# High and low products in runs, and the bias rows by way of DRAM: a two-layer decoder trunk

## The chip, the core and the metric

The kernel runs on one core of a Trainium2 chip. The metric is the device time of one execution in microseconds. Five engines work side by side, each through its own queue in order: PE multiplies matrices (with PEld, its weight loads), DVE and ACT do elementwise work, POOL small things, SP and ACT issue DMAs. All weights come from HBM, 173 MB in one execution.

## The reference, cut to what matters

Two layers, 256 positions, width 1024. Each layer is a half-step feed-forward, a mixer of three head groups, and a second half-step feed-forward:

```
def swiglu(x, w_gate, w_up, w_down):
    return (jax.nn.silu(x @ w_gate) * (x @ w_up)) @ w_down      # 1024 -> 2816 -> 1024

for l in range(DEPTH):                                          # DEPTH = 2
    h = x + 0.5 * swiglu(rms_norm(x, ffn1_norm[l]), ffn1_gate[l], ffn1_up[l], ffn1_down[l])
    u = rms_norm(h, mix_norm[l]);  z = u @ w_in[l]
    ...                       # differential attention, short convolution, RG-LRU
    h = h + jnp.concatenate([y_da, y_sc, y_lru], axis=-1) @ w_out[l]
    x = h + 0.5 * swiglu(rms_norm(h, ffn2_norm[l]), ffn2_gate[l], ffn2_up[l], ffn2_down[l])
return rms_norm(x, final_norm)
```

The attention adds a bias to its logits that depends on the distance of query and key alone: `rel_bias[t5_bucket(distance)]`, eight heads' worth.

## The kernel before

**Split products.** Every float32 operand is split into a high part (rounded to the matrix engine's format) and a low part, the rest. A product is then high by high, high by low and low by high. ACT makes a weight chunk's high part `wh` (line 161), DVE its low part `wl` by subtraction (line 165), each in two halves of four contraction tiles; the activations lie in `xx` (feed-forward input) and `hid` (hidden), high and low side by side, so that one matmul with `wh` and 512 columns takes both, and one with `wl` and 256 columns takes the high half alone. `wide` (line 219) issues this pair for one contraction tile k: first `wh`, then `wl`, and for the last tile of a sum in the other order. The 512 result columns are added afterwards.

**Stages.** A feed-forward has 22 chunks for gate and up in turn (`up_gate`, line 311), each with two output columns a and b (`ga`, `gb`, `ua`, `ub`) of eight tiles k, by `wide_col` (line 228): 44 columns of 16 matmuls in a pass, four passes in all. Three of the four then go through `ffn` (line 380): four blocks n of two columns `da`, `db`, each over 22 tiles k that come in three chunks of 8, 8 and 6 tiles. The mixer's projections (`col`, line 213) are in 256-column matmuls throughout, and the last down projection (`row`, line 840) in matmuls of 512 and of 256 columns, each kind in a row.

**Order.** The schedule is by hand: each engine gets its instructions in the order in which the Python code issues them. `chunk` (line 196) and `pump` (line 190) keep ACT and DVE some chunks ahead of PE with four buffers of `wh` and of `wl`, and SP's loads three ahead of those.

**Bias.** Hooks run behind chunk pair c of the first pass (line 808). Hook 2, `bias_rows`, makes the eight bias rows of 384 values (`br`, on 8 partitions of SBUF). Hook 7, `skew_out`, writes each row 128 times into DRAM (`skew`, 1536 KB) from ACT's queue; hook 9, `skew_in`, reads it back with a shifted stride into `bias`, which the attention needs much later. An instruction behind `skew_in` on ACT cannot start before ACT has waited for `skew` to land.

Of the kernel before, what the change touches and what calls it, by code (L numbers as in the profile page):

```python
# [11 lines left out]
F32 = mybir.dt.float32  # L12
# [5 lines left out]
P = 128  # L18
DEPTH = 2
S = 256  # L20
D = 1024
KD = D // P
DFF = 2816
KF = DFF // P
# [45 lines left out]
def trunk(ctx: ExitStack, tc: tile.TileContext, t, out):  # L70
    nc = tc.nc
# [7 lines left out]
    dr = ctx.enter_context(tc.tile_pool(name="dr", bufs=1, space=bass.MemoryType.DRAM))  # L79
# [4 lines left out]
    def pair(name):  # L84
        return [bank(name + "a"), bank(name + "b")]
# [4 lines left out]
    def flat(ap):  # L90
        return ap.rearrange("p a b -> p (a b)")
# [10 lines left out]
    xx = cst.tile([P, KD, 2, S], F32R, name="xx")  # L102
# [5 lines left out]
    bias = cst.tile([P, 8, S], F32, name="bias")  # L108
# [12 lines left out]
    for l in range(DEPTH):  # L121
        for f in ("ffn1", "ffn2"):
# [3 lines left out]
            w = t[f"{f}_down{l}"]  # L126
# [69 lines left out]
    def chunk(held=0):  # L196

        n = st["use"]
        st["live"] = n - held
        while st["split"] < 2 * (n + 1):  # L200
            split_half()
        low_to(2 * (n + 1))
        load_to(n + LS + LD)
        st["use"] += 1
        return parts.pop(n)
# [10 lines left out]
        for k in ks:  # L216
            mm3(o, w[0][:, k - k0, c], w[1][:, k - k0, c], vh[:, k], vl[:, k], k == first, k == last)

    def wide(o, wh, wl, v, first, last):

        if last:
            nc.tensor.matmul(o[:, :S], lhsT=wl, rhs=v[:, 0], start=first, stop=False)
            nc.tensor.matmul(o, lhsT=wh, rhs=flat(v), start=False, stop=True)
        else:
            nc.tensor.matmul(o, lhsT=wh, rhs=flat(v), start=first, stop=False)  # L225
            nc.tensor.matmul(o[:, :S], lhsT=wl, rhs=v[:, 0], start=False, stop=False)  # L226

    def wide_col(o, w, i, ks):
        c = slice(i * P, (i + 1) * P)
        for k in ks:  # L230
            wide(o, w[0][:, k, c], w[1][:, k, c], xx[:, k], k == 0, k == KD - 1)

    def fresh_cols(norm, b, column):

# [145 lines left out]
    def ffn(norm, first, gain, hooks=()):  # L380
        hid = up_gate(norm, first, hooks)
        for n in range(4):
            acc = pair("d")
            for k0, k1 in DOWN_K:
                w = chunk()
                for i in range(2):
                    c = slice(i * P, (i + 1) * P)
                    for k in range(k0, k1):
                        wide(acc[i], w[0][:, k - k0, c], w[1][:, k - k0, c], hid[k], k == 0, k == KF - 1)
                    if k1 == KF:  # L390
                        settle(2 * n + i, acc[i], gain, norm)
                    if n < 3 or k1 < KF or i == 1:
                        pump()


    kept = {}
# [63 lines left out]
    def bias_rows():  # L460
# [2 lines left out]
        kept["br"] = wk.tile([8, 384], F32, tag="at", name="br")  # L463
        nc.vector.tensor_copy(out=kept["br"], in_=b[:8, :384])

    def skew_out():
        kept["skew"] = dr.tile([8, P, 384], F32, name="skew")
        nc.scalar.dma_start(out=kept["skew"], in_=kept["br"].unsqueeze(1).to_broadcast([8, P, 384]))

    def skew_in():  # L470
        sk = kept["skew"][:]
        nc.scalar.dma_start(
            out=bias, in_=bass.AP(sk.tensor, sk.offset + P - 1, [[383, P], [P * 384, 8], [1, S]])
        )


    def mixer(l, norm):
# [327 lines left out]
        nc.gpsimd.tensor_tensor(out=xq, in0=junk[:, 0], in1=junk[:, 1], op=ALU.add)  # L805

    norm = Norm()
    ffn(norm, True, ("mix_norm", 0), {1: constants_in, 2: bias_rows, 4: exponents, 5: softplus, 6: factors, 7: skew_out, 9: skew_in})
    for l in range(DEPTH):
        norm = Norm()  # L810
        mixer(l, norm)
        norm = Norm()
        if l < DEPTH - 1:
            ffn(norm, False, ("ffn1_norm", l + 1))
            norm = Norm()
# [13 lines left out]
    hid = up_gate(norm, False, {2 + 2 * k + n: turn_back(k, n) for k in range(2) for n in range(2)})  # L829
# [7 lines left out]
    acc = (f0, f1 + [bank("f2")])  # L837
# [41 lines left out]
    for c in range(NC - 2):  # L879
        w = chunk()  # L880
# [4 lines left out]
    w = [chunk(), chunk(1)]  # L885
# [45 lines left out]
```

## Time and profile before

| | |
|---|---|
| median of 3 runs | 963.83 us (963.38 to 964.7) |
| the profiled execution | 963.61 us |
| its span, first to last instruction | 961.5 us |
| PE busy | 950.6 us, 99% of the span |
| DVE, ACT busy | 682.7 us (71%), 548.8 us (57%) |
| matmuls, all of them | 5894 |

A matmul's busy time contains its way through the pipeline (a 512-column one shows about 0.40 us though the next begins after 0.23), so a busy PE says only that it never ran dry. How fast it goes is read from the distance between the starts of successive matmuls, best over whole columns, whose times stand with two decimals. The two kinds of matmul are called h (with `wh`, 512 columns) and l (with `wl`, 256 columns) from here on.

### The profile page before, as it was taken

The page shows a single profiled execution, that of the slowest core. Times are in us where ns is not written, and L with a number is a line of the kernel's source. Part 1 is how long each engine was busy: PE and PEld are TensorE (multiplying, and loading weights), DVE is VectorE, ACT ScalarE, POOL GpSimd, SP SyncE. Part 2 cuts the span into 40 slices and gives each one's busy share as a digit, 9 for nine tenths or more (in the row PEclk, how much of TensorE's full clock was granted, in tenths as well). Part 3 has the DMA queues.
Part 4 walks back from the last instruction along what each step waited for, and adds up shares of the span by engine and source line. Part 5 has one row for each costly group of instructions (what it writes and reads, how often), then busy time and mean ns, then how long its engine had stood idle before and what let it go on. Part 6 is the DMA issues. An engine that isn't in the chain of part 4 may idle for free.

```text
span 961.5 us, 14717 instructions
## 1 busy us (share of the span) xinstructions
PE 950.6 (99%) x5894; PEld 849.5 (88%) x5894; DVE 682.7 (71%) x1018; ACT 548.8 (57%) x935; POOL 27.5 (3%) x49
## 2 busy tenths in 40 slices
PE   8999999999999999999999999999999999999997
PEld 7888878899999888888888888888999988888886
DVE  6788647767787877765678777575778777777643
ACT  7467436557766655554556555454677666555431
POOL 2003000000000000000000000000000000000000
PEclk9999999999999999999999999999999999999999
DMA  7665767554445655553646554454633555555721
GB/s 275 233 217 178 180 213 254 170 190 155 140 167 176 219 180 197 192 193 131 241 145 220 200 186 165 164 199 173 218 133 132 176 194 200 176 176 181 277 89 44
DMA packets 29671, 176.67 MB, mean 184 GB/s; under 512 B 4227, under 2 KB 6308, under 8 KB 10404
## 3 DMA queue, kind: packets, MB, share of 16 engines
q1 hardware_dynamic: 25632, 171.45, 51.2%
q10 hardware_dynamic: 3972, 4.29, 2.1%
q8 instruction: 46, 0.75, 0.3%
q14 instruction: 21, 0.17, 0.1%
HBM read 173.11 MB, written 2.62 MB: 183 GB/s over the span
## 4 chain that ended last, share of the span: by engine, by line
PE 79%; DVE 7%; DMA 5%; ACT 5%; issue 2%; POOL 1%; ACTq 0%; SPq 0%; POOLq 0%; DVEq 0%
PE db L225 6%; PE da L225 6%; PE gb L225 6%; PE ub L225 6%; PE ua L225 6%; PE ga L225 6%; DMA skew<-br 4%; PE db L226 3%; PE da L226 3%; PE ga L226 3%; PE ua L226 3%; PE gb L226 3%; PE ub L226 3%; DVE wl L165 3%; ACT wh L161 2%
## 5 line engine op out<-in xcount | busy, mean ns | idle before, releaser
L165 DVE TENSOR_TENSOR wl<-raw,wh 128x1024 fp32r<-128x1024 f32 (+2 forms) x334 | 390.6, 1196 | 63.5 <-ACT wh L161 63.2
L161 ACT ACTIVATE wh<-raw 128x1024 fp32r<-128x1024 f32 (+2 forms) x334 | 325.4, 1021 | 49.1 <-PE f L211 21.1
L225 PE MATMUL ga<-xx,wh 128*128 128x512 f32 x308 | 111.9, 401 | 0.8 <-DVE xx L307 0.8
L225 PE MATMUL gb<-xx,wh 128*128 128x512 f32 x308 | 111.3, 399 | 0.0
L225 PE MATMUL ub<-xx,wh 128*128 128x512 f32 x308 | 110.7, 399 | 0.0
L225 PE MATMUL ua<-xx,wh 128*128 128x512 f32 x308 | 110.3, 397 | 0.0
L225 PE MATMUL da<-hid,wh 128*128 128x512 f32 x252 | 89.8, 394 | 0.4 <-ACT wh L161 0.4
L225 PE MATMUL db<-hid,wh 128*128 128x512 f32 x252 | 89.8, 395 | 0.0
L226 PE MATMUL ga<-xx,wl 128*128 128x256 f32 x308 | 87.2, 283 | 0.8 <-DVE wl L165 0.8
L226 PE MATMUL gb<-xx,wl 128*128 128x256 f32 x308 | 86.6, 281 | 0.0
L226 PE MATMUL ua<-xx,wl 128*128 128x256 f32 x308 | 86.5, 281 | 0.0
L226 PE MATMUL ub<-xx,wl 128*128 128x256 f32 x308 | 86.3, 280 | 0.0
L226 PE MATMUL da<-hid,wl 128*128 128x256 f32 x252 | 70.8, 281 | 1.7 <-DVE wl L165 1.7
L226 PE MATMUL db<-hid,wl 128*128 128x256 f32 x252 | 70.6, 280 | 0.0
L225 PEld LDWEIGHTS ga<-xx,wh 128*128 128x128 f32 x308 | 58.4, 189 | 13.5 <-ACT wh L161 1.0
L225 PEld LDWEIGHTS gb<-xx,wh 128*128 128x128 f32 x308 | 58.2, 189 | 12.4
L225 PEld LDWEIGHTS ub<-xx,wh 128*128 128x128 f32 x308 | 57.9, 188 | 12.1
L225 PEld LDWEIGHTS ua<-xx,wh 128*128 128x128 f32 x308 | 58.0, 188 | 11.8
L226 PEld LDWEIGHTS ga<-xx,wl 128*128 128x128 f32 x308 | 58.6, 190 | 3.5 <-DVE wl L165 2.0
L335 ACT ACTIVATE sg<-sg 128x512 f32<-128x512 f32 x44 | 27.8, 633 | 57.7 <-DVE sg L334 57.7
L226 PEld LDWEIGHTS gb<-xx,wl 128*128 128x128 f32 x308 | 58.5, 190 | 1.8
L226 PEld LDWEIGHTS ub<-xx,wl 128*128 128x128 f32 x308 | 58.2, 189 | 1.9
(313 smaller groups left out, 1988.3 us busy)
## 6 DMA issues: line engine op xcount, KB each, us to landing
raw<-in_ffn_up SPq DMA_DIRECT2D x43, 1024.0 KB, 4.8
raw<-in_ffn_gate SPq DMA_DIRECT2D x42, 1024.0 KB, 4.7
raw<-in_ffn_down SPq DMA_DIRECT2D x35, 1024.0 KB, 4.8
raw<-in_w_in SPq DMA_DIRECT2D x22, 1024.0 KB, 4.8
raw<-in_ffn_down SPq DMA_DIRECT2D x12, 768.0 KB, 4.1
raw<-in_w_out SPq DMA_DIRECT2D x8, 1024.0 KB, 4.8
skew<-br ACTq DMA_DIRECT2D x1, 1536.0 KB
xT<-in_x SPq DMA_DIRECT2D x4, 256.0 KB, 4.9
```

Source lines behind the costliest of these rows:

```text
L161: nc.scalar.activation(out=parts[i][0][:, s], in_=raws[i][:, s], func=AF.Copy)
L165: nc.vector.tensor_tensor(out=lo[:, s], in0=raws[i][:, s], in1=h[:, s].bitcast(F32), op=ALU.subtract)
L225: nc.tensor.matmul(o, lhsT=wh, rhs=flat(v), start=first, stop=False)
L226: nc.tensor.matmul(o[:, :S], lhsT=wl, rhs=v[:, 0], start=False, stop=False)
L335: nc.scalar.activation(out=s, in_=s, func=AF.Silu)
```

## The change

`wide` now takes a list of tiles and an order. With order "hl" it issues all h of the list and then all l; with "lh" the other way round. `wide_col` makes two such runs of four tiles, k 0 to 3 as "hl" and k 4 to 7 as "lh". In the down projection a run is a whole chunk of 8, 8 or 6 tiles: "lh" for the last chunk, and for column b of the middle one, "hl" else. The number of matmuls, their operands and their sizes stay.

The bias rows first go to a small DRAM buffer `rows` (new hook 3), and the 128 copies are made from there, into a `skew` whose outer dimension is the 128 copies and no more the eight rows. Lines 219 to 231, 387 to 389, 466 to 474 and 808:

```diff
-    def wide(o, wh, wl, v, first, last):
-        if last:
-            nc.tensor.matmul(o[:, :S], lhsT=wl, rhs=v[:, 0], start=first, stop=False)
-            nc.tensor.matmul(o, lhsT=wh, rhs=flat(v), start=False, stop=True)
-        else:
-            nc.tensor.matmul(o, lhsT=wh, rhs=flat(v), start=first, stop=False)
-            nc.tensor.matmul(o[:, :S], lhsT=wl, rhs=v[:, 0], start=False, stop=False)
+    def wide(o, w, i, v, ks, k0, first, last, order):
+        c = slice(i * P, (i + 1) * P)
+        for what in order:
+            for k in ks:
+                if what == "h":
+                    nc.tensor.matmul(o, lhsT=w[0][:, k - k0, c], rhs=flat(v[k]), start=k == first, stop=k == last)
+                else:
+                    nc.tensor.matmul(o[:, :S], lhsT=w[1][:, k - k0, c], rhs=v[k][:, 0], start=False, stop=False)
     def wide_col(o, w, i, ks):
-        c = slice(i * P, (i + 1) * P)
-        for k in ks:
-            wide(o, w[0][:, k, c], w[1][:, k, c], xx[:, k], k == 0, k == KD - 1)
+        v = [xx[:, k] for k in range(KD)]
+        for run, order in (([k for k in ks if k < 4], "hl"), ([k for k in ks if k >= 4], "lh")):
+            wide(o, w, i, v, run, 0, 0, KD - 1, order)
...
-                    c = slice(i * P, (i + 1) * P)
-                    for k in range(k0, k1):
-                        wide(acc[i], w[0][:, k - k0, c], w[1][:, k - k0, c], hid[k], k == 0, k == KF - 1)
+                    wide(acc[i], w, i, hid, range(k0, k1), k0, 0, KF - 1, "lh" if k1 == KF or i == 1 and k0 > 0 else "hl")
...
+    def rows_out():
+        kept["rows"] = dr.tile([8, 384], F32, name="rows")
+        nc.scalar.dma_start(out=kept["rows"], in_=kept["br"])
     def skew_out():
-        kept["skew"] = dr.tile([8, P, 384], F32, name="skew")
-        nc.scalar.dma_start(out=kept["skew"], in_=kept["br"].unsqueeze(1).to_broadcast([8, P, 384]))
+        kept["skew"] = dr.tile([P, 8, 384], F32, name="skew")
+        r = kept["rows"][:]
+        nc.scalar.dma_start(out=kept["skew"], in_=bass.AP(r.tensor, r.offset, [[0, P], [384, 8], [1, 384]]))
...
-            out=bias, in_=bass.AP(sk.tensor, sk.offset + P - 1, [[383, P], [P * 384, 8], [1, S]])
+        nc.scalar.dma_start(out=bias, in_=bass.AP(sk.tensor, sk.offset + P - 1, [[8 * 384 - 1, P], [384, 8], [1, S]]))
...
+        1: constants_in, 2: bias_rows, 3: rows_out, 4: exponents, 5: softplus, 6: factors, 7: skew_out, 9: skew_in
```

What stands in a row on PE from the fifth tile of an up column (`ua`) to the start of the next (`ub`), before:

```order
L225 MATMUL ua<-xx,wh_261 128x512
L226 MATMUL ua<-xx,wl_262 128x256
L225 MATMUL ua<-xx,wh_261 128x512
L226 MATMUL ua<-xx,wl_262 128x256
L225 MATMUL ua<-xx,wh_261 128x512
L226 MATMUL ua<-xx,wl_262 128x256
L222 MATMUL ua<-xx,wl_262 128x256
L223 MATMUL ua<-xx,wh_261 128x512
L225 MATMUL ub<-xx,wh_261 128x512
L226 MATMUL ub<-xx,wl_262 128x256
```

And two whole columns in the same pass now (x4 and x8 are that many in a row):

```order
L226 MATMUL ga<-xx,wh_302 128x512 x4
L228 MATMUL ga<-xx,wl_303 128x256 x8
L226 MATMUL ga<-xx,wh_302 128x512 x4
L226 MATMUL gb<-xx,wh_302 128x512 x4
L228 MATMUL gb<-xx,wl_303 128x256 x8
L226 MATMUL gb<-xx,wh_302 128x512 x4
```

Where h and l took turns within a column, eight l now stand in a row, and across two columns eight h.

On PE in block n = 0 of the first down projection, first two chunks, now (before, they alternate as above; `hid` is in three pieces, whose numbers stand behind the name):

```order
L226 MATMUL da<-hid_117,wh_1224 128x512 x8
L228 MATMUL da<-hid_117,wl_1225 128x256 x8
L226 MATMUL db<-hid_117,wh_1224 128x512 x8
L228 MATMUL db<-hid_117,wl_1225 128x256 x8
L226 MATMUL da<-hid_117,wh_1275 128x512 x2
L226 MATMUL da<-hid_118,wh_1275 128x512 x6
L228 MATMUL da<-hid_117,wl_1276 128x256 x2
L228 MATMUL da<-hid_118,wl_1276 128x256 x6
L228 MATMUL db<-hid_117,wl_1276 128x256 x2
L228 MATMUL db<-hid_118,wl_1276 128x256 x6
L226 MATMUL db<-hid_117,wh_1275 128x512 x2
L226 MATMUL db<-hid_118,wh_1275 128x512 x6
```

Runs are 8 long here, and 16 where columns a and b meet with the same kind; with the third chunk a block has five runs of l.

On ACT, at hook 7, before:

```order
L340 ACTIVATE hid_118<-ga 128x2x256
L468 DMA skew<-br 1024x1x384
L161 ACTIVATE wh_1074<-raw_955 128x1024 x2
L328 ACTIVATE sg<-ga 128x256
L328 ACTIVATE sg<-gb 128x256
```

And now:

```order
L343 ACTIVATE hid_118<-ga 128x2x256
L475 DMA skew<-rows 128x3072
L161 ACTIVATE wh_1076<-raw_957 128x1024 x2
L331 ACTIVATE sg<-ga 128x256
L331 ACTIVATE sg<-gb 128x256
```

The place in ACT's queue is the same; the source is now DRAM, and the transfer is laid out as 128 rows of 3072 values where it was 1024 rows of 384. The new `rows_out` stands four hooks ahead, behind the `hid` of chunk pair 3.

## Rows read from the trace of the kernel before

**Rows 1.** The page: busy time by engine, granted clock by slice.

```profile
PE 950.6 (99%) x5894; PEld 849.5 (88%) x5894; DVE 682.7 (71%) x1018; ACT 548.8 (57%) x935; POOL 27.5 (3%) x49
PEclk9999999999999999999999999999999999999999
```

**Rows 2.** Windows: stretch, length, busy and count by engine, clock, DMA: 38 columns, 18 columns.

```profile
315.17:422.33 107.16, 107.16 (x609) 93.20 (x608) 80.95 (x108) 61.51 (x98) 0.00 (x0) 1.00 0.56 190
843.68:894.44 50.76, 50.76 (x289) 44.13 (x288) 37.09 (x49) 28.62 (x45) 0.00 (x0) 1.00 0.56 193
```

**Rows 3.** Windows: three half columns of down; 48 matmuls of the mixer.

```profile
440.65:448.97 8.32, 8.32 (x50) 7.34 (x49) 6.10 (x8) 5.47 (x7) 0.00 (x0) 1.00 0.85 280
212.04:217.80 5.76, 5.76 (x50) 5.76 (x49) 5.41 (x10) 5.74 (x7) 0.00 (x0) 1.00 0.79 287
```

**Rows 4.** Timeline of PE in the last projection: start, length; first matmuls of four outputs, and of the next chunk.

```profile
899.96 0.40 PE L209 MATMUL f0a<-wh,hid 128*128 128x512 f32 x1
...
901.35 0.39 PE L209 MATMUL f0b<-wh,hid 128*128 128x512 f32 x1
...
902.71 0.39 PE L209 MATMUL f1a<-wh,hid 128*128 128x512 f32 x1
...
904.07 0.28 PE L209 MATMUL f1b<-wh,hid 128*128 128x256 f32 x1
...
905.50 0.40 PE L209 MATMUL f0a<-wh,hid 128*128 128x512 f32 x1
```

**Rows 5.** Timeline of PE where the last up column meets the last projection.

```profile
894.21 0.40 PE L223 MATMUL ub<-xx,wh 128*128 128x512 f32 x1
894.44 0.40 PE L209 MATMUL f0a<-wh,hid 128*128 128x512 f32 x1
...
895.81 0.39 PE L209 MATMUL f0b<-wh,hid 128*128 128x512 f32 x1
```

**Rows 6.** Windows: blocks n = 0 and 1 of the first down projection, n = 1 of the second.

```profile
134.92:153.29 18.37, 16.28 (x89) 13.45 (x88) 11.79 (x16) 9.88 (x15) 0.00 (x0) 1.00 0.77 242
153.29:168.82 15.53, 15.53 (x90) 13.48 (x88) 11.21 (x19) 7.78 (x13) 0.00 (x0) 1.00 0.74 260
437.87:453.17 15.30, 15.30 (x90) 13.45 (x89) 9.86 (x15) 7.67 (x13) 0.00 (x0) 1.00 0.55 190
```

**Rows 7.** Timeline of ACT around the copies of the bias rows, with idle time and releaser.

```profile
103.26 0.81 ACTq L468 DMA_DIRECT2D skew<-br  x1
...
124.95 2.01 ACT L161 ACTIVATE wh<-raw 128x1024 fp32r<-128x1024 f32 x2 [10.16 <-DMA raw<-in_ffn_up]
...
139.49 0.40 ACTq L472 DMA_DIRECT2D bias<-skew  x1
139.99 2.01 ACT L161 ACTIVATE wh<-raw 128x1024 fp32r<-128x1024 f32 x2 [6.24 <-DMA skew<-br]
```

**Rows 8.** SP's loads at line 154: issue to landing, issued 45 to 95 us, then 95 to 150.

```profile
DMA to landing us min/median/max: 4.7/4.7/6.7
...
DMA to landing us min/median/max: 4.7/12.9/19.1
```

**Rows 9.** DMA issues: how often, KB, us from issue to landing.

```profile
bd<-in_final_norm ACTq DMA_DIRECT2D x1, 512.0 KB, 3.6
```

**Rows 10.** Timeline of PE in the first pass, column ga of chunk pair 1.

```profile
19.09 0.40 PE L225 MATMUL ga<-xx,wh 128*128 128x512 f32 x1
19.68 0.39 PE L226 MATMUL ga<-xx,wl 128*128 128x256 f32 x1 [0.19 <-DVE wl L165]
...
21.91 0.39 PE L226 MATMUL ga<-xx,wl 128*128 128x256 f32 x1 [0.56 <-DVE wl L165]
...
23.19 0.50 PE L259 MATMUL ssq<-ones,xq 128*128 128x1 f32 x4
```

**Rows 11.** PE's waits: who for whom, us in total, times, longest.

```profile
PE da L226 <- DVE wl L165: 1.7, 2, 0.9
...
PE ga L226 <- DVE wl L165: 0.8, 2, 0.6
PE da L225 <- ACT wh L161: 0.4, 1, 0.4
```

More of the change, by code (lines that the diff above doesn't have):

```diff
@@ L464, in bias_rows @@
         nc.vector.tensor_copy(out=kept["br"], in_=b[:8, :384])
+    def rows_out():
+        kept["rows"] = dr.tile([8, 384], F32, name="rows")
+        nc.scalar.dma_start(out=kept["rows"], in_=kept["br"])
     def skew_out():
-        kept["skew"] = dr.tile([8, P, 384], F32, name="skew")
-        nc.scalar.dma_start(out=kept["skew"], in_=kept["br"].unsqueeze(1).to_broadcast([8, P, 384]))
+        kept["skew"] = dr.tile([P, 8, 384], F32, name="skew")
+        r = kept["rows"][:]
+        nc.scalar.dma_start(out=kept["skew"], in_=bass.AP(r.tensor, r.offset, [[0, P], [384, 8], [1, 384]]))
     def skew_in():
         sk = kept["skew"][:]
-        nc.scalar.dma_start(
-            out=bias, in_=bass.AP(sk.tensor, sk.offset + P - 1, [[383, P], [P * 384, 8], [1, S]])
-        )
+        nc.scalar.dma_start(out=bias, in_=bass.AP(sk.tensor, sk.offset + P - 1, [[8 * 384 - 1, P], [384, 8], [1, S]]))
     def mixer(l, norm):
@@ L807, in trunk @@
     norm = Norm()
-    ffn(norm, True, ("mix_norm", 0), {1: constants_in, 2: bias_rows, 4: exponents, 5: softplus, 6: factors, 7: skew_out, 9: skew_in})
+    once = {
+        1: constants_in, 2: bias_rows, 3: rows_out, 4: exponents, 5: softplus, 6: factors, 7: skew_out, 9: skew_in
+    }
+    ffn(norm, True, ("mix_norm", 0), once)
     for l in range(DEPTH):
```

## The prediction, made before the changed kernel ran

> **What bounds the kernel now.** I read the page first. PE is busy for 99% of the span, with nines for the granted clock in all 40 slices, the upper of its two levels, 2.4 GHz [rows 1], so the time is the sum of PE's steps from one matmul's start to the next, plus the few places where it waits. The waits come next: on weights that ACT or DVE have not finished, `wide` waits at five places in the whole program, four for `wl` and one for `wh` [rows 11]. They are one column at the start [rows 10] and block n = 0 of the first down projection [rows 6]. So two questions are left: how long a pair of h (512 columns) and l (256 columns) takes, and what those few waits cost.
>
> For the pair I went to windows over whole columns. In the gate/up passes 38 columns take 107.16 us and 18 take 50.76 us: 2.820 us a column, 0.3525 a pair [rows 2]. In a stretch of the down projection with the same strict alternation, 24 pairs take 8.32 us, 0.3467 a pair [rows 3]. The same two instructions thus run at two paces. What is the least? The mixer's 48 matmuls of 256 columns take 5.76 us, 0.1200 each [rows 3]; in the last projection `f0b`, six matmuls of 512 columns, goes from 901.35 to 902.71, 0.2267 each [rows 4]. Sum 0.3467: the good pace is simply both at their least, and a column's least is 8 x 0.3467 = 2.773. The gate/up passes pay 0.047 more on each column, with no wait on another engine in the records.
>
> **Part 1, the runs: what a change of size costs.** The last projection shows it, since it goes round from 512 to 256 columns and back in each chunk. Coming from 256, the first six of 512 (`f0a`) take 901.35 - 899.96 = 1.39 us where `f0b` takes 1.36: 0.03 more, over a few matmuls. The twelve of 256 after `f1a` take 905.50 - 904.07 = 1.43 where twelve at 0.120 are 1.44: 0.01 less. The whole round (18 of 512, 12 of 256) is 5.54 against 4.08 + 1.44 = 5.52 at the least. So a round trip costs 0.02 [rows 4]. The only other entry is milder: the seven of 512 from 894.21 to 895.81 take 1.60 against 1.587 [rows 5], which with the 0.01 given back leaves about 0.006. Runs that never settle are the other end: the column's last h to the first of the next output takes 894.44 - 894.21 = 0.23 [rows 5], and rounding leaves up to 0.235. I take 0.02, since the new columns too enter h after a long run of l, as `f0a` does.
>
> Gate/up: a column now has one round trip instead of fifteen switches: 2.773 + 0.02 = 2.793 for 2.820, 0.027 less. Four passes of 44 columns make 176; I leave out four in each, at the starts, where hooks, the norm and a fresh `xx` cut the columns up, and count 160. Gain 160 x 0.027 = **4.3 us** (0.6 if h stays at 0.235 and l at 0.117, which is what then remains of today's pair: 8 x 0.352 = 2.816; 6.6 at 0.006 a round trip).
>
> Down: a block is 44 pairs, 15.25 at the least. It takes 15.53 in slow blocks and 15.30 in fast ones, of which a row each stands in [rows 6]; of the twelve blocks five are slow (three of the first pass and the first of each later one) and seven fast. The new order has five round trips in a block: 15.25 + 0.10 = 15.35. Gain 5 x 0.18 - 7 x 0.05 = **0.5 us** (1.2 at 0.006; a loss of about 1 at unsettled steps, since the fast blocks would slow down).
>
> Does the order make PE wait for weights? In an up column `wl` of the first half is needed about 0.7 us later than now, `wh` of the second half later too, and `wl` of the second half 0.23 us sooner (eight earlier steps of 0.227 and 0.120 instead of four pairs and an h). In the last down chunk `wl` comes first, 0.23 sooner. PE's waits on weights are nil outside the two places named [rows 11], so 0.23 costs nothing where DVE is more than that ahead, which I take everywhere but there. It does cost in the start column [rows 10]: DVE delivers the second half of `wl` at 21.91, and from there PE now needs four l and four h, where before one h was already done: 0.23 us later. The first wait, 19.09 to 19.68, is covered by the three h that now come first, but that only lengthens the second. **Loss 0.2 us** (0 to 0.5). The last matmul of each column and of each block is an h as before, so nothing behind it starts later.
>
> **Part 2, the bias copies.** Here a wait ends in PE. ACT issues the 1536 KB `skew` at 103.26, and its read-back at 139.49; for 6.24 us ACT does nothing but wait for `skew` to land, with the next `wh` halves queued behind [rows 7]. The transfer also crowds SP's loads: these land in 4.7 us before it and in up to 19.1 beside it [rows 8], and ACT had lost 10.16 us to one of them [rows 7]. PE runs dry in block n = 0: 18.37 us against 15.53 of its neighbour, 2.84 us [rows 6], the waits for `wl` and `wh` on `da` and `db` [rows 11] with the weight loads' restart behind each. The new copy starts at the same place in ACT's queue. No row shows DRAM copied to DRAM. The nearest is the final gain, one DRAM row copied to 128 partitions, 512 KB in 3.6 us [rows 9]: three times that size, 10.8 us. From the other side, nothing changes: 36.2 us from issue to the end of the wait [rows 7]. With 10.8 it lands at 114; without the late load ACT would reach `skew_in` around 126, when the ninth pair is stored (PE ends pair 9 some 11 us ahead of the block at 134.92, a pair being four columns). So there are about 12 us to spare, and it may take 23 before ACT waits at all. **Gain 2.84 us**, and nothing is late behind it: ACT's `wh` and DVE's `wl` then run as in the other blocks.
>
> What the trace shows of that copy is 1536 KB in 36.2 us. The Trainium skill (DMA: Bandwidth & Descriptors, "Why a DMA increments its semaphore by 16 and not by 1") says that a copy is spread over the largest number of engines up to 16 that divides the slowest dimension of both sides: eight with the eight rows outermost, sixteen with the 128 copies. By that alone the time would halve to an estimated 18 us, still before 126, so the sum would be the same.
>
> `rows_out` adds one 12 KB DMA issue to ACT at hook 3. Behind it stand the next `wh` halves; an ACT issue takes 0.40 to 0.81 us [rows 7], and no matmul waits for `wh` there [rows 11]. It waits for `br`, made a hook earlier, and `skew_out` waits for it four hooks (some 45 us) later. Cost 0; if ACT had no lead, 0.8.
>
> **The sum**, on the profiled execution: 963.61 (span 961.5 and 2.1 around it) - 4.3 - 0.5 + 0.2 - 2.84 = **956.2 us**. The median of the runs is 963.83, 0.2 above the profiled one and well within the runs' spread of 1.3, so I leave it.
>
> **Rivals.** *The order changes nothing on PE* (each step hangs on its own size): only part 2 counts, 963.61 - 2.84 + 0.2 = 961.0. For it: no wait is visible in the passes. Against it: the same pairs at 0.3525 and 0.3467 [rows 2, 3]. [...] Chance 0.10.
> *The runs don't settle*: h stays at 0.235 and l at 0.117, 0.352 a pair. Gain 0.6, down loses 1: 963.61 - 2.84 - 0.6 + 1.0 + 0.2 = 961.4. For it: the 0.23 to 0.24 of every h that follows a change [rows 4, 5]. Against: `f0b`, which shows them settled. Chance 0.07.
> *The copy stays slow* (DRAM writes bound, not the source): the stall stays, 956.2 + 2.84 = 959.0. Chance 0.06.
> *Slower*: a run of h with a new weight each time lets every load of 512-column work show. Until now h is followed by l, whose load lies under a long step; in a run nothing else differs but the weights, and `f0b` uses one weight for two of its three steps. The longest step that two decimals show for an h is 0.24 (`f0a`, 899.96 to 900.20). With every h at 0.24 and l at 0.12, a pair is 0.36: 1408 pairs lose 0.0075 and 528 of the down projection some 0.01, together 16 us, so 963.61 + 16 - 2.84 + 0.2 = 977. It ends slower once a pair exceeds the present mean of about 0.3515 by (2.84 - 0.2)/1936 = 0.0014. Against it: the mixer's l change weights at 0.120, and every third step of `f0b` does at 0.227. Chance 0.05.
>
> **How the numbers follow.** Forecast 956.2 with chance 0.72; its own bounds (0.006 a round trip; an uncovered 0.8 on ACT and half the gain in the passes) reach from 953 to 959. That with the slow copy is 0.78; to leave out no more than 2 in 10 the range must take in the first rival, 961.0. Range 953.0 to 961.0. A measurement of this kernel can tell about 0.2%, 1.9 us, from no change: faster is below 961.7. Forecast, slow copy and first rival lie below, the unsettled runs about half: faster 0.88, same 0.07, slower 0.05.
>
> **What would show it.** Regular gate/up columns of 2.79 us; steps of 0.227 and 0.120 within the runs from the fifth matmul on; blocks of the down projection at 15.35 all alike, n = 0 too; `skew` landed before 126 and no ACT wait before `wh` behind `skew_in`; loads beside it at 5 to 8 us; the start column's second wait longer by about 0.5 and its end 0.2 later. Columns at 2.82 mean the first rival, at 2.81 the unsettled runs, above 2.83 the last; a stall around 140 us the slow copy.

## The result, and the profile after

The changed kernel takes 957.21 us (median of 4 runs, 955.71 to 957.42), the one before 963.81 in the same set: ratio 0.9927, with an interval of 0.9910 to 0.9944. Forecast were 956.2 us, faster, within 953.0 to 961.0. The profiled run took 957.42 us, with a span of 955.3 (before: 963.61 and 961.5), so the two profiled spans differ by 6.2 us.

The page of the changed kernel: first the busy time by engine (to set beside [rows 1]), then the chain of work that ended last, as shares of the span by engine.

```profile
PE 944.3 (99%) x5894; PEld 850.2 (89%) x5894; DVE 683.0 (71%) x1018; ACT 549.6 (58%) x935; POOL 27.6 (3%) x49
...
PE 91%; ACT 3%; DVE 2%; issue 1%; DMA 1%; POOL 0%; SPq 0%; POOLq 0%; ACTq 0%; DVEq 0%
```

The same number of matmuls keeps PE busy for 6.3 us less, and PE's idle time (10.9 and 11.0 us) is the same: a stall has gone and idle time at the start has come. Where, shows stage by stage when the starts of the same matmuls are set beside each other (timeline of PE, both profiles):

| First matmul of | before, us | after, us | gained since the line above |
|---|---|---|---|
| the first up column | 13.46 | 14.37 | -0.91 |
| the norm's first sum, behind the start column `ga` | 23.19 | 24.25 | -0.15 |
| the first down projection | 134.92 | 135.04 | 0.94 |
| the mixer | 199.65 | 196.46 | 3.31 |
| the second down projection (mixer, gate/up pass 2) | 422.33 | 418.14 | 1.00 |
| the third down projection (down 2, pass 3) | 608.56 | 603.40 | 0.97 |
| the last projection (down 3, mixer, pass 4) | 894.44 | 888.30 | 0.98 |
| the last output, `f` | 953.90 | 947.76 | 0.00 |

Four gate/up passes give 3.9 us, the first down projection 3.3, and the first 24 us take 1.06 back.

Windows of the changed kernel (stretch, length, busy time and count by engine, granted clock, DMA share and GB/s): 38 gate/up columns; blocks n = 0 and 1 of the first down projection; n = 1 of the second.

```profile
312.00:418.14 106.14, 106.14 (x609) 93.42 (x608) 80.98 (x108) 61.57 (x98) 0.00 (x0) 1.00 0.56 191
135.04:150.40 15.36, 15.36 (x89) 13.52 (x88) 7.36 (x10) 5.42 (x8) 0.00 (x0) 1.00 0.46 163
150.40:165.75 15.35, 15.35 (x89) 13.52 (x88) 9.94 (x15) 7.67 (x13) 0.00 (x0) 1.00 0.55 189
433.50:448.85 15.35, 15.35 (x89) 13.52 (x88) 9.85 (x15) 7.67 (x13) 0.00 (x0) 1.00 0.56 189
```

The first row answers [rows 2]: 106.14 / 38 = 2.793 us a column, where it was 2.820. The other three answer [rows 6]: blocks of 18.37, 15.53 and 15.30 us have become three of 15.35 or 15.36: the first two take 3.01 and 0.18 less, the third 0.05 more. In block n = 0 PE's busy time is now the whole window; before, 2.1 us of it were idle.

One column on PE's timeline (start, length of the group, and how many matmuls), with the next column's first matmul:

```profile
312.00 1.07 PE L226 MATMUL ua<-xx,wh 128*128 128x512 f32 x4
312.91 1.12 PE L228 MATMUL ua<-xx,wl 128*128 128x256 f32 x8
313.86 1.09 PE L226 MATMUL ua<-xx,wh 128*128 128x512 f32 x4
314.79 0.39 PE L226 MATMUL ub<-xx,wh 128*128 128x512 f32 x1
```

From start to start, the first four h take 0.91 (0.2275 each), eight l 0.95 (0.119 each), and the four h that follow them 0.93. Going from one kind to the other and back costs 0.02 in all, in the four h behind the l (0.93 against 4 x 0.2267 = 0.91).

ACT around the copies of the bias rows (timeline, with idle time and its releaser), to set beside [rows 7]:

```profile
104.10 0.58 ACTq L475 DMA_DIRECT2D skew<-rows  x1
...
125.68 0.40 ACTq L479 DMA_DIRECT2D bias<-skew  x1
126.21 2.00 ACT L161 ACTIVATE wh<-raw 128x1024 fp32r<-128x1024 f32 x2
```

The page's row of that copy (KB, median us from issue to landing):

```profile
skew<-rows ACTq DMA_DIRECT2D x1, 1536.0 KB, 8.6
```

And SP's loads at line 154 that were issued between 95 and 150 us, beside the second line of [rows 8]:

```profile
DMA to landing us min/median/max: 4.2/5.2/10.7
```

The copy lands 8.6 us behind its issue, 13 us before ACT issues the read-back. ACT's `wh` behind the read-back has no idle time in front of it, where 6.24 us stood; the read-back itself comes 13.8 us earlier. Of these 7.45 are ACT's earlier arrival: the `hid` in front of the read-back starts at 125.67, where it started at 133.12, because a late load holds ACT up for 2.28 us and no more for 10.16. The other 6.36 are the wait for the copy.

Last, PE's waits (who for whom, us in all, times, longest), beside [rows 11]:

```profile
PE ga L228 <- DVE wl L165: 1.9, 4, 1.2
...
PE ga L226 <- ACT wh L161: 0.7, 1, 0.7
```

None for `da` is left. Both rows belong to the first 24 us, where the time was given back.

### The profile page after: what moved, and what is told of

It reads as the page before. It is cut to its first block, busy times and chain, and to the rows that moved or that the text cites. A ratio compares the mean times of both kernels' runs of the same rounds, so it can differ in the third digit from the quotient of the medians.

```text
span 955.3 us, 14718 instructions
## 1 busy us (share of the span) xinstructions
PE 944.3 (99%) x5894; PEld 850.2 (89%) x5894; DVE 683.0 (71%) x1018; ACT 549.6 (58%) x935; POOL 27.6 (3%) x49
## 4 chain that ended last, share of the span: by engine, by line
PE 91%; ACT 3%; DVE 2%; issue 1%; DMA 1%; POOL 0%; SPq 0%; POOLq 0%; ACTq 0%; DVEq 0%
PE gb L226 8%; PE ua L226 8%; PE ub L226 8%; PE ga L226 8%; PE db L226 6%; PE da L226 6%; PE gb L228 4%; PE ua L228 4%; PE ub L228 4%; PE ga L228 4%; PE db L228 3%; PE da L228 3%; ACT wh L161 1%; PE wb L211 1%; PE wb L210 1%
## 5 line engine op out<-in xcount | busy, mean ns | idle before, releaser
L226 PE MATMUL ub<-xx,wh 128*128 128x512 f32 x352 | 95.6, 393 | 0.0
L226 PEld LDWEIGHTS ga<-xx,wh 128*128 128x128 f32 x352 | 62.8, 189 | 13.6 <-ACT wh L161 2.3
L226 PE MATMUL db<-hid,wh 128*128 128x512 f32 x264 | 66.7, 392 | 0.0
L226 PE MATMUL da<-hid,wh 128*128 128x512 f32 x264 | 66.4, 391 | 0.0
L343 ACT ACTIVATE hid<-ga 128x512 fp32r<-128x512 f32 x44 | 27.8, 633 | 54.3 <-DVE ga L341 54.3
L226 PEld LDWEIGHTS da<-hid,wh 128*128 128x128 f32 x264 | 48.0, 189 | 9.0
L226 PEld LDWEIGHTS db<-hid,wh 128*128 128x128 f32 x264 | 47.3, 189 | 8.3
L228 PE MATMUL ga<-xx,wl 128*128 128x256 f32 x352 | 51.2, 283 | 1.9 <-DVE wl L165 1.9
L344 DVE TENSOR_TENSOR hid<-ga,hid 128x512 fp32r<-128x512 f32 x44 | 30.5, 693 | 30.8 <-ACT hid L343 30.8
L292 ACT ACTIVATE xx<-xT,pc 128x256 fp32r<-128x256 f32 x40 | 20.5, 512 | 54.0 <-DVE xT L287 35.8
L228 PEld LDWEIGHTS ua<-xx,wl 128*128 128x128 f32 x352 | 48.0, 190 | 3.5
```

The costliest lines, as they stand in the source:

```text
L226: nc.tensor.matmul(o, lhsT=w[0][:, k - k0, c], rhs=flat(v[k]), start=k == first, stop=k == last)
L228: nc.tensor.matmul(o[:, :S], lhsT=w[1][:, k - k0, c], rhs=v[k][:, 0], start=False, stop=False)
L292: nc.scalar.activation(out=xh[:, d], in_=x, func=AF.Copy, scale=g)
L343: nc.scalar.activation(out=h[:, :, 0], in_=a, func=AF.Copy)
L344: nc.vector.tensor_tensor(out=h[:, :, 1], in0=a, in1=h[:, :, 0].bitcast(F32), op=ALU.subtract)
```

## The experiments

Two questions had to be told apart: how much each part gives alone, and what it is in each part that gives. The changed kernel ran again in the set of the first two and of the pairs. The kernel before took 963.40 us in that set, and 963.66 and 963.54 in the two later ones. Three of the experiments are single runs.

**The change again.** 

> The changed kernel once more, as the yardstick of this set. Theory (the gain is steady, and the 0.9 us by which its first profile lagged behind the sum came from loads that landed late at the start): regular gate/up columns of 2.793 us and blocks of the down projection of 15.35 us again, to the nanosecond; the first up column starts anywhere between 13.4 and 14.5 us; the time is 955.5 to 957.5. Rival (the start is slower by the change itself, since from tile 4 on l stands ahead of h there): the first up column starts at 14.3 us or later again, and the time is 957 or more.

Measured: 957.11 us (956.83 to 957.18) against 963.40 for before, ratio 0.9931 (0.9916 to 0.9946); columns at 2.793 and blocks at 15.35 and 15.36 once more. The first up column starts at 14.17: this falls in the theory's range, and the time also in the rival's, so the run does not decide between them.

### Each part alone

**The order without the DRAM buffer.** The old copy from `br`, its layout and its hooks:

```diff
-    def rows_out():
-        kept["rows"] = dr.tile([8, 384], F32, name="rows")
-        nc.scalar.dma_start(out=kept["rows"], in_=kept["br"])
-        kept["skew"] = dr.tile([P, 8, 384], F32, name="skew")
+        kept["skew"] = dr.tile([8, P, 384], F32, name="skew")
+        nc.scalar.dma_start(out=kept["skew"], in_=kept["br"].unsqueeze(1).to_broadcast([8, P, 384]))
...
```

> The new order of products, with the bias copies as in the kernel before. Theory (the two parts add up): 4.8 us of 0.047 to 0.020 a column and of equal blocks, less 0.2 at the start, so 959.0 to 960.3; block n = 0 of the first down projection keeps its stall of 2 to 3 us, ACT waits 6 us for the copies, and all other columns are at 2.793. Rival (order costs nothing, part 2 brought everything): 963.5 to 964. Rival (the runs of eight h give ACT and DVE the time they lack, so that the stall shrinks with the order alone): block n = 0 below 16.5 us, time below 958.5.

Measured: 961.23 us (960.43 to 962.34), ratio 0.9977 (0.9967 to 0.9986): 2.2 us gained, less than expected. Windows of this kernel, blocks n = 0 and 1 of the first down projection:

```profile
134.74:154.37 19.63, 16.15 (x89) 13.58 (x88) 13.11 (x18) 9.90 (x15) 0.00 (x0) 1.00 0.76 236
154.37:169.72 15.35, 15.35 (x89) 13.52 (x88) 10.47 (x17) 7.77 (x13) 0.00 (x0) 1.00 0.71 253
```

The stall is 19.63 - 15.35 = 4.28 us, where it was 2.84 under the old order. PE's timeline in that block, the three groups that wait:

```profile
141.52 2.14 PE L226 MATMUL da<-hid,wh 128*128 128x512 f32 x8 [1.06 <-ACT wh L161]
...
145.39 0.74 PE L228 MATMUL da<-hid,wl 128*128 128x256 f32 x4 [1.26 <-DVE wl L165]
...
150.43 0.62 PE L228 MATMUL da<-hid,wl 128*128 128x256 f32 x3 [1.16 <-DVE wl L165]
```

Up to the last chunk the stall is as long as under the old order: the two chunks before it take 14.02 us (134.74 to 148.76) where the next block's take 11.15, 2.87 more, and in before 14.16 (134.92 to 149.08) where the next block's take 11.30, 2.86 more. The wait in the last chunk is the one that is new (in before both waits for `wl`, 0.77 and 0.94, stand in the second chunk), and nearly all of the 1.44 us falls there: that chunk now begins with l, and there the `wl` in question is the last weight to be made. In the old order an h stood in front of each l and gave DVE time. Some of it is a later copy: ACT gets past its wait at 140.41 here, 5.67 us behind the block's start, against 5.07 in before (139.99 behind 134.92, [rows 6, 7]), and all that follows it is 0.6 later too. That without this the new wait would be 0.6 shorter is argued; no run shows it.

**The DRAM buffer without the order.** `wide` as in before, one h and one l in turn:

```diff
-        for what in order:
-            for k in ks:
+        if last:
+            nc.tensor.matmul(o[:, :S], lhsT=wl, rhs=v[:, 0], start=first, stop=False)
+            nc.tensor.matmul(o, lhsT=wh, rhs=flat(v), start=False, stop=True)
+        else:
+            nc.tensor.matmul(o, lhsT=wh, rhs=flat(v), start=first, stop=False)
+            nc.tensor.matmul(o[:, :S], lhsT=wl, rhs=v[:, 0], start=False, stop=False)
...
```

> The bias rows by way of DRAM, with the products in the order of the kernel before. Theory: only the stall goes, 2.84 us, so 960.5 to 961.5; block n = 0 takes 15.5 us like its neighbours, gate/up columns stay at 2.820, and the copies land in under 12 us. Rival (the copies' crowding of the loads cost more than the stall, or the new copies crowd them as well): under 960, or block n = 0 still above 16.5.

Measured: 960.77 us (960.14 to 960.96), ratio 0.9969 (0.9957 to 0.9980): 2.6 gained. Windows of blocks n = 0 and 1:

```profile
135.66:151.19 15.53, 15.53 (x89) 13.48 (x88) 7.44 (x10) 5.43 (x8) 0.00 (x0) 1.00 0.46 162
151.19:166.49 15.30, 15.30 (x89) 13.45 (x88) 9.94 (x15) 7.68 (x13) 0.00 (x0) 1.00 0.55 190
```

The stall is gone and the two paces of the old order are still there; the columns stay at 2.82 and the copy lands in 8.8 us. So the faster copy is worth 2.6 under the old order (963.40 against 960.77) and 4.1 under the new one (961.23 against 957.11). Each part alone gives 2.2 and 2.6, both give 6.3. The parts don't add up, because the order makes the stall dearer and the copy removes the stall whole.

### What makes the copy fast

**Eight rows outermost.** The source stays in DRAM, but the transfer has the old shape:

```diff
-        kept["skew"] = dr.tile([P, 8, 384], F32, name="skew")
+        kept["skew"] = dr.tile([8, P, 384], F32, name="skew")
-        ... in_=bass.AP(r.tensor, r.offset, [[0, P], [384, 8], [1, 384]]))
+        ... in_=bass.AP(r.tensor, r.offset, [[384, 8], [0, P], [1, 384]]))
...
```

> The changed kernel, with the copies made from the DRAM buffer as now, but laid out as before, the eight rows outermost and 128 copies of each. Theory (the layout decides how many DMA engines share the work, eight or sixteen): the copies take twice the 8.8 us or more, loads beside them land late again (over 10 us), and if it is over 22 us ACT waits behind the read-back. Rival (the source decides, eight partitions of SBUF before and DRAM now): under 10 us, loads at 5 to 8 us, no wait. Time as the changed kernel's, 955.5 to 957.5, unless the copies take over 25 us, then up to 4 us more.

Measured: 957.42 us, one run: nothing lost. Loads beside the copy land in 4.8 to 7.7 us, so the expected late loads did not come. Windows of 8 us from 104 us on (last column: GB/s), of before and then of this kernel:

```profile
104.00:112.00 8.00, 8.00 (x47) 6.94 (x46) 7.10 (x9) 5.46 (x8) 0.00 (x0) 1.00 0.66 131
112.00:120.00 8.00, 8.00 (x48) 6.96 (x47) 2.94 (x4) 1.01 (x2) 0.00 (x0) 1.00 0.72 151
```

```profile
104.00:112.00 8.00, 8.00 (x48) 7.08 (x47) 6.75 (x10) 6.10 (x9) 0.00 (x0) 1.00 0.75 264
112.00:120.00 8.00, 8.00 (x48) 6.99 (x47) 5.81 (x9) 3.57 (x6) 0.00 (x0) 1.00 0.85 303
```

ACT's queue from the copy's issue to the read-back (packets, MB, time as a share of 16 engines), in this kernel:

```profile
q10 hardware_dynamic: 1032, 1.57, 19.4%
```

and in the changed kernel, whose copy is 128 packets of 12 KB instead of 1024 of 1.5 KB:

```profile
q10 hardware_dynamic: 144, 1.57, 26.1%
```

By the packet records the copy runs for 34.4 us in before (from `br` in SBUF, 1024 packets), 13.6 here (from DRAM, the same 1024 packets) and 6.8 in the changed kernel. So the layout is a factor of two, and the larger step, 2.5 times, is the source. With this copy the core moves 264 and 303 GB/s in the same 16 us (267 and 313 in the changed kernel), where it moved 131 and 151 while the old copy ran: the source on eight SBUF partitions also kept the other loads slow. A copy of 13.6 us still has 6.5 us to spare (its last packet ends at 119.3, the read-back is issued at 125.8), so the layout gives nothing here. The Trainium skill (DMA: Bandwidth & Descriptors, "Why a DMA increments its semaphore by 16 and not by 1") has a copy use the largest number of engines up to 16 that divides the slowest dimension of both sides; with 8 and then 128 that is eight and sixteen. The trace agrees with it: 13.6 and 6.8 us, and 8 and 16 small packets beside the 1024 and 128 of the two copies. The packets also grew eightfold, so that the engines alone make the factor is not shown. Nothing in that rule tells a source in SBUF from one in DRAM, so it leaves the 34.4 us open.

### What a change of size costs

**Runs of two** in the gate/up columns (h2 l4 h4 l4 h2):

```diff
-        for run, order in (([k for k in ks if k < 4], "hl"), ([k for k in ks if k >= 4], "lh")):
-            wide(o, w, i, v, run, 0, 0, KD - 1, order)
+        for j in range(4):
+            wide(o, w, i, v, [k for k in ks if k // 2 == j], 0, 0, KD - 1, "lh" if j % 2 else "hl")
```

> The changed kernel with runs of two tiles in gate/up (h h l l l l h h h h l l l l h h), so two round trips of sizes in a column with runs of four. Theory (each change to h costs its first four or five steps 0.007, 0.008, 0.002, 0.005, 0.005, and each change to l gives 0.007 back): 2 x 0.015 a column, 2.803 us, 1.5 us over the changed kernel. Rival (0.020 for each round trip, whatever the run): 2.813, 3.2 us over. Rival (short runs stay in the slow pace of the alternation): 2.82, 4.3 us over.

Measured: 958.79 us, one run. The window of 38 columns:

```profile
311.88:418.53 106.65, 106.65 (x610) 93.20 (x608) 80.93 (x108) 61.46 (x98) 0.00 (x0) 1.00 0.55 191
```

2.8066 a column: 0.033 above the least for two round trips, 0.017 each, between the two expected prices. In runs of four a round trip costs nearly what it costs in runs of eight or twelve.

**Strict turns everywhere**, h then l for every tile, in the projections of both kinds:

```diff
-        for run, order in (([k for k in ks if k < 4], "hl"), ([k for k in ks if k >= 4], "lh")):
-            wide(o, w, i, v, run, 0, 0, KD - 1, order)
+        for k in ks:
+            wide(o, w, i, v, (k,), 0, 0, KD, "hl")
...
```

> The changed kernel with strict alternation of h and l throughout, the last tile of a column included, so that no two of a kind ever stand together. Theory (the slow pace of the kernel before is entered where two l and two h meet at a column's end, and strict alternation, once settled, keeps to 0.3467 a pair): gate/up columns of 2.773 us after the first of a pass, blocks of 15.25, and 951.5 to 954. Rival (a stretch keeps the pace at which it was entered, and the passes are entered at the slow one): columns of 2.82 to 2.83 throughout, 961 to 963. Rival (operands decide, xx slow and hid fast): gate/up 2.82, blocks 15.25, 960 to 961.5.

Measured: 956.58 us, one run, no slower than the changed kernel. None of the three expectations holds for the whole kernel: the least pace stands in some passes and the slow one in others. Windows: 30 columns of the first gate/up pass, then 40 of the second.

```profile
47.59:132.39 84.80, 84.80 (x483) 73.53 (x481) 70.17 (x109) 53.89 (x86) 8.53 (x18) 1.00 0.66 225
307.32:418.25 110.93, 110.93 (x642) 97.00 (x641) 85.19 (x114) 65.74 (x104) 0.00 (x0) 1.00 0.57 198
```

The same instructions in the same order take 84.80 / 30 = 2.827 us a column in one pass and 110.93 / 40 = 2.773, the least, in the next, at a granted clock of 1.00 in both. Column by column the trace shows where the pace changes. Up to 41 us columns without a wait take 2.773; then the small matmuls on `bt` come in between, and from 47.59 on every column takes 2.82 to 2.83, through the whole first down projection too. In passes 2 and 3 all are at 2.773, once the norm's own matmuls are past. In the last pass the transposes come in between, and behind them it is 2.83 to the end. So a strictly alternating stretch keeps the pace at which it was entered, and an interruption can change it. It is not the operands, since `xx` and `hid` each run at both. Against the kernel with the DRAM buffer and the old order (960.77), only the last pair of each column and block differs: before turned it round (l h), so that two l and then two h met at each column's end, and its regular gate/up columns took 2.820 in all four passes. Without that, passes 2 and 3 are at the least. Turns aren't dear in themselves; what the runs buy is that the pace no longer depends on the entry, for 0.02 a column.

The Trainium skill (TensorE: Matmul & The Clock Gate, "Back-to-back issue gap") gives N/2.4 + 2.5 ns as the isolated gap of one matmul, from which an estimated 0.325 us for an h and an l follows, and says that in a stream the weight loads set the spacing too. The trace has 0.3467 and 0.353 for the same pair, so neither pace is that estimate.

### A better order

**Both columns of a chunk share the runs**: h16 l16 for a pair of columns, one round trip for two columns; in down two round trips a block instead of five.

```diff
+    def wide_pair(o, w, v, ks, k0, first, last, order, between=None):
+        for n, what in enumerate(order):
+            for i in range(2):
+                for k in ks:
+                    ...
-                    wide(acc[i], w, i, hid, range(k0, k1), k0, 0, KF - 1, ...)
+                wide_pair(acc, w, hid, range(k0, k1), k0, 0, KF - 1, "hl" if k0 == 0 else "lh", mid)
```

> The changed kernel with longer runs: the two columns of a chunk share their runs, sixteen h and then sixteen l in gate/up, and in the down projection h, l l, h and then l, h of its three chunks, so that a pair of columns has one round trip instead of two, and a block two instead of five. Theory (what is left over is 0.020 for each round trip of sizes): two columns take 2 x 2.773 + 0.020 = 5.567 for 5.587, 80 times, 1.6 us; blocks 15.25 + 0.04 = 15.29 for 15.35, 12 times, 0.7 us; and the wait in the second chunk pair is covered by sixteen h, 1.4 us: 3 to 4 us under the changed kernel, 952.5 to 954.5. Rival (the cost depends on the number of matmuls since the change, growing with the run): two columns at 5.587 or more, gain under 1.5 us. Rival (the later need of the low parts, or the common end of both columns, makes PE wait elsewhere, at a chunk or at a norm): new waits of 0.3 us or more in the records of PE.

Measured: 954.35 us (953.92 to 954.57), ratio 0.9903 (0.9888 to 0.9917). PE's timeline, one pair of columns and the start of the next:

```profile
305.36 2.00 PE L244 MATMUL ga<-xx,wh 128*128 128x512 f32 x8
307.20 1.98 PE L244 MATMUL gb<-xx,wh 128*128 128x512 f32 x8
309.02 1.11 PE L246 MATMUL ga<-xx,wl 128*128 128x256 f32 x8
309.97 1.12 PE L246 MATMUL gb<-xx,wl 128*128 128x256 f32 x8
310.93 2.00 PE L244 MATMUL ua<-xx,wh 128*128 128x512 f32 x8
```

310.93 - 305.36 = 5.57 for two columns (2 x 2.773 + 0.02), and a block of down takes 15.29 (15.25 + 0.04). 88 pairs at 0.02 less and 12 blocks at 0.06 less make 2.5 of the 2.8 us that this kernel gains on the changed one. In the first pass a wait has moved: the late `wl` is covered by sixteen h now, but PE then waits for the norm's `dg`:

```profile
27.05 0.68 PE L284 MATMUL rb<-dg,ones 128*128 128x128 f32 x4 [1.02 <-DVE dg L271]
```

**The same, with the norm's spread half a chunk later**, and pairs in the first chunk too:

```diff
                 def mid(j):
-                        if first and c == 1:
-                            (norm.ssq, norm.spread)[j // 2]()
+                        if first and c == 1 and j == 1:
+                            norm.ssq()
...
+                    if first and c == 1:
+                        norm.spread()
+                        gate(s)
+                        store(0, s, a)
```

> The paired runs, with the norm's row spread, and the gate that needs it, half a chunk later in the first pass, and with both h of a tile pair before its l at the start. Theory (what was left of the paired version's loss is one wait of PE for the norm's diagonal, 1.18 us at 25.7): that wait is gone, the rest is as it was: 1.0 to 1.4 us under the paired runs, 952.7 to 953.6. Rival (the wait moves on, since DVE has the same work and is what is late there): a wait of 0.5 us or more turns up within the next two chunks, and the gain is under 0.6 us.

Measured: 955.87 us (953.98 to 957.05), ratio 0.9923 (0.9906 to 0.9940), no gain on the pairs and more spread. The wait for `dg` is gone, and another has come. PE's timeline first, then ACT's queue:

```profile
43.72 0.80 PE L488 MATMUL bt<-oneh,rb 33*8 33x384 f32 x2 [1.85 <-DMA rb<-in_rel_bias]
```

```profile
41.17 0.39 ACTq L432 DMA_DIRECT2D rb<-in_rel_bias  x1
```

ACT issues the load of `rb` only at 41.17, one hook ahead of the matmul that needs it, and PE is there by 41.9. Why the runs spread by 3 us was not looked into; the profiled one is the fastest.

**And the bias matmul one hook later:**

```diff
+    def fourth():
+        exponents()
+        rows_out()
-        1: constants_in, 2: bias_rows, 3: rows_out, 4: exponents, 5: softplus, 6: factors, 7: skew_out, 9: skew_in
+        1: constants_in, 3: bias_rows, 4: fourth, 5: softplus, 6: factors, 7: skew_out, 9: skew_in
```

> The paired runs with the norm's spread late and both h first at the start, and the bias rows' product one hook later (hook 3, their way to DRAM hook 4). Theory (the 2.0 us that PE waited at 41.6 was for the constants' loads, which ACT had issued only 1 us earlier, at the end of its backlog): that wait is gone and nothing takes its place, 951.5 to 954.5 by the start's loads, a median 1.5 to 2 us under the version with the rows at hook 2 (955.87). Rival (ACT's backlog itself is what PE meets, at the next weights): a wait of 0.5 us or more between 42 and 60, and a median above 954.5.

Measured: 952.87 us (952.38 to 952.92) against 963.54, ratio 0.9887 (0.9871 to 0.9904): the fastest of all. What is left of PE's waits:

```profile
PE warm L811 <- DVE ones L803: 1.0, 1, 1.0
PE ga L244 <- DVE xx L324: 1.0, 1, 1.0
```

Both end with the first column's first matmul or earlier. No wait on a weight is listed any more.

**The same with the first chunk tile by tile**, as in the changed kernel:

```diff
-            wide_pair(b, parts[0], [xx[:, k] for k in range(KD)], range(2 * j, 2 * j + 2), 0, 0, KD - 1, "hl")
+            for k in range(2 * j, 2 * j + 2):
+                for i in range(2):
+                    wide_col(b[i], parts[0], i, (k,))
```

> The same with the start tile by tile as in the changed kernel (from tile 4 on l before h). Theory (the start is bound by the loads' landing, the order there is worth 0.2 us at most): within 0.4 us of the version with both h first. Rival (h first covers the late low parts at the start): 0.5 us slower or more, with waits for wl between 8 and 12 us.

Measured: 953.05 us (952.13 to 953.39), ratio 0.9889 (0.9874 to 0.9904). No difference that can be measured: the order in the first chunk decides nothing.

## Why the prediction held, and where its terms were off

**The gate/up columns.** The least of 2.773 plus one round trip at 0.02 was put at 2.793; it is 2.793. The four passes gave 3.9 us for the 4.3 forecast. The second pass gained 1.03 (124.89 to 123.86 us from its first column to the down projection), where 40 times 0.027 is 1.08: its 38 regular columns gave 1.02 (107.16 to 106.14), and the six around the norm next to nothing, where four had been left out. Runs of two confirm the price of the round trip, 0.017. The rival in which the runs don't settle is out: the steps are 0.227 and 0.120 inside the runs, and what a change of size adds is confined to the four h behind an l. So is the one in which every h with new weights costs 0.24. The rival in which the order changes nothing is out by the order alone, 2.2 us with a dearer stall.

But the reason for the old price was only half seen. The prediction took 0.3525 a pair as the price of fifteen switches in a column. The kernel with strict turns has as many and shows two paces, by how a stretch was entered. The forecast didn't rest on that, because the runs have a price of their own.

**The down blocks.** 15.35 all alike was forecast and is what all three windows show. The three down projections went from 64.73, 61.44 and 61.43 us to 61.42, 61.42 and 61.41, 3.35 less with the stall; the two terms were 0.5 + 2.84 = 3.34.

**The copy.** It was put at 10.8 us by three times the final gain's time [rows 9]; it takes 8.6. The 12 us to spare are 13. Loads beside it land in up to 10.7 us, not 8, and one of them keeps ACT waiting for 2.3 us without reaching PE. The rival of a copy that stays slow is out.

**Two sums beside the forecast** don't come out as written. At 0.006 a round trip a block would take 15.28 and the down projections would gain 5 x 0.25 + 7 x 0.02 = 1.4, not 1.2; and the chances listed for faster, with half of the unsettled runs, add up to 0.915, not 0.88. The forecast stands on neither, and with 1.4 its own lower bound is still 953 (956.2 - 2.3 - 0.9).

**What was missed about the two parts:** the sum adds them as if each had its price by itself. It came out right only because both were made: with the order alone the stall would have cost 4.28 instead of 2.84, where the expectation for that run still had it at its old price. The loss that the prediction looked for where l comes first, "0.23 sooner", was looked for in places with DVE ahead; in block n = 0, where DVE is late, it came on top.

**The start** is the term that was mis-sized: 0.2 forecast, 1.06 in the profile. Of it the start column itself, from the first up column to the norm's sum, is 9.88 against 9.73 us: 0.15, as forecast. PE's timeline there, beside [rows 10]:

```profile
19.98 1.07 PE L226 MATMUL ga<-xx,wh 128*128 128x512 f32 x4
20.89 0.63 PE L228 MATMUL ga<-xx,wl 128*128 128x256 f32 x4
22.75 0.74 PE L228 MATMUL ga<-xx,wl 128*128 128x256 f32 x4 [1.22 <-DVE wl L165]
23.32 1.09 PE L226 MATMUL ga<-xx,wh 128*128 128x512 f32 x4
```

One wait of 1.22 stands where there were two of 0.19 and 0.56: the first is covered and the second longer, as the prediction had it. The other 0.91 lies ahead of that, in the first chunk, about which the prediction has no term. ACT's and PE's timeline now:

```profile
8.41 0.63 ACT L161 ACTIVATE wh<-raw 128x512 fp32r<-128x512 f32 x1 [1.43 <-DMA raw<-in_ffn_gate]
```

```profile
9.10 0.51 PE L226 MATMUL ga<-xx,wh 128*128 128x512 f32 x1 [0.69 <-ACT wh L161]
9.82 0.39 PE L228 MATMUL ga<-xx,wl 128*128 128x256 f32 x1 [0.22 <-DVE wl L165]
...
10.98 0.28 PE L228 MATMUL gb<-xx,wl 128*128 128x256 f32 x1
11.47 0.39 PE L228 MATMUL ga<-xx,wl 128*128 128x256 f32 x1 [0.20 <-DVE wl L165]
```

And PE in before, up to the same matmul as the first of these:

```profile
8.38 0.63 PE L225 MATMUL gb<-xx,wh 128*128 128x512 f32 x1
8.81 0.41 PE L226 MATMUL gb<-xx,wl 128*128 128x256 f32 x1
9.03 0.63 PE L225 MATMUL ga<-xx,wh 128*128 128x512 f32 x1
```

A load of the first weights came late: ACT made this `wh` at 8.41, and at 6.75 in before's profile. Yet the h that needs it starts only 0.07 later than in before, 9.10 against 9.03, because before's first matmuls step at 0.43 and 0.21 us, about twice their least, while the new ones step at 0.23 and 0.12 and then stand and wait. The 0.84 left arise between that h and the first up column: 5.27 us (9.10 to 14.37) against 4.43 (9.03 to 13.46), with waits for the late `wl` behind that h and again at tile 4, where the new order puts l first. The kernel with the old order and the new copy has the same late load (`wh` at 8.33) and takes 4.92 there (9.12 to 14.04); the repetition of the changed kernel, with `wh` at 8.40, takes 5.08 (9.09 to 14.17). So some 0.5 goes with the late load, and 0.16 to 0.35 may go with the order.

The first up column starts at 14.01, 14.17, 14.37 and 14.47 in the four profiles with this order and at 13.46 and 14.04 in two with the old one, but not for one reason. In the two extremes of the new order the load is hardly the cause: the profile of 14.01 (the order alone) has the slow steps up to 10.1, like before, and in the profile of 14.47 (eight rows outermost) the clock falls, behind waits of PE of 1.32 and 0.23 us for its first operands. Windows of before, then of that run:

```profile
7.00:8.00 1.00, 1.00 (x4) 0.90 (x5) 1.00 (x3) 0.39 (x1) 0.00 (x0) 1.00 0.91 289
```

```profile
9.00:10.00 1.00, 1.00 (x4) 0.85 (x4) 0.73 (x3) 1.00 (x3) 0.00 (x0) 0.50 1.06 379
```

The second shows a granted clock of 0.50, the lower level of 1.2 GHz, and four matmuls in 1 us. The first prints 1.00 and has the same four in 1 us; that PE ran at the lower level there too is argued from these steps, and not shown by the clock. The last experiment says that the order of the first chunk is worth nothing measurable under pairs. What the load's landing and the pace of the first matmuls depend on stays open. This 0.9 and the 0.4 of the gate/up passes are about the difference between 956.2 and 957.42.

**Rows to ACT.** `rows_out` at nothing held: no matmul waits for `wh` between its hook and the copy.

## What to carry to other kernels

When one engine is busy for 99%, read its steps from start to start, by size, in several stretches: one pair of instructions at two prices says there is something to gain that no wait shows. Group matmuls of one size into runs as long as the data allow, across output columns too (strict turns reached the least as well, but only in stretches that were entered well), and then look at what the longer lead uncovers, because each wait taken away brought the next one into view. Price two parts of a change together wherever one decides what the other's wait can hide behind.

## What was not expected of the hardware

- Matmuls of 512 and 256 columns in strict turns have two paces, 0.3467 and about 0.353 us a pair, at the same granted clock; a stretch keeps the one at which it was entered, over hundreds of pairs, and small matmuls or transposes in between can change it. What in the engine holds it is not shown.
- A round trip between the sizes costs 0.017 to 0.02 us whether the runs are four, eight or twelve long.
- Copying eight rows 128 times into DRAM, 1.5 MB, took 34.4 us out of eight SBUF partitions and 13.6 out of DRAM with the same number and size of packets, and the core's traffic in the same 16 us went from 131 and 151 to 264 and 303 GB/s.
